# Encoder layer on one core: loads where the MLP begins, low parts of the activations, and the second product block by block

## The chip, the cores and the metric

The kernel runs on one core of one Trainium2 chip. The metric is the device time of one execution in microseconds (us). Before the change the median of three runs is 1813.73 us (1812.82 to 1814.87).

The engines are named as the profile names them: PE is TensorE's matmul stream, PEld its weight loads, DVE is VectorE, ACT is ScalarE, POOL is GpSimd and SP is SyncE, which issues all DMA transfers here.

## The reference, cut to what matters

One encoder layer is applied to two groups of tokens, 512 and 1024 of them, with shared weights, all in float32.

```python
def _layer(h, ...):
    a = _rmsnorm(h, norm_mix_g)
    z = a @ w_in                                  # queries, keys, values, pooling input
    ...
    h = h + jnp.concatenate([o_attn, o_pool], axis=-1) @ w_out
    m = _rmsnorm(h, norm_mlp_g)
    h = h + jnp.square(jax.nn.relu(m @ w_up)) @ w_down      # 1024 -> 4096 -> 1024
    gate = jax.nn.sigmoid(_rmsnorm(h, norm_ple_g) @ w_ple_gate)
    h = h + gate * (p_i @ w_ple_proj)
    return h
```

A final RMSNorm follows. The change touches the line of the MLP and what leads to it.

## The kernel before

**Tiles and stages.** The 1536 tokens are three chunks of 512 (c = 0, 1, 2). Activations stand transposed: 128 features on the partitions, tokens along the free dimension, so the residual `hT[c]` of a chunk is four tiles of [128, 2, 512]. Every float32 operand of a product is split into a high and a low part, and `three` gives the three matmuls high x high, high x low and low x high. The stages are: input projection (to about 196 us), attention and pooling with the output projection woven in (to 579 us), the MLP (to about 1620 us), the gate and the final norm.

**Buffers.** Nearly all tiles come from one pool of 49 buffers, `slot`. A tile takes a buffer that an earlier tile has left, and its first writer then waits for the last reader of that earlier tile. Where that reader was a DMA, the writer waits for the DMA's semaphore. PE, ACT, DVE and POOL run their instructions in the order in which the code is written. SP's queue is put in order when the program is built. Its transfers count on eight semaphores in turn, DMAHW0 to DMAHW7, and each transfer waits for the one eight places earlier.

**Ahead of the MLP.** `heads_out(p)` adds the output projection of a block of 256 tokens to `hT` (L755); p = 4 and 5 belong to chunk 2 and are the last of the stage. When a chunk is done, the chore `spill(c)` writes `hT[c]` to DRAM (`h_d`, L708), for chunk 2 after 16 empty steps. The chore `make_m(c)` (L595) reads it back, prepares the operand `mo` of the up product and the mean square of the rows plus epsilon, a [128, 512] tile that here is called the divisor `w`; L647 writes that to DRAM (`w_d`). Chores are generators: `step()` runs one of them by one step.

**The MLP.** A `Pair` (c, g) handles two of the 32 blocks of 128 hidden features for one chunk; 16 pairs for each chunk. Its up product uses seven products instead of eight (a Strassen form): `product(i)` for i = 1, 6, 2, 5, 7, 3, 4 with weight parts w1 to w7 and banks `px`, `py`, `pz`, `pq`. DVE reads the banks into u2 (L858), u4 (L866) and the activations c1, c2 (L870, L874, L880). Products 3 and 4 add onto `pz` and `pq` and thus wait for those reads. ACT takes relu and square and gives the high part of the activations r (L876, L882); DVE subtracts for the low part (L886). `down(a)` (L828) is the second product: two output blocks e = 0, 1 of a bank pair `pd`, each summed over the pair's two input blocks f = 0, 1, and then added to `hT` (L837). The `down` calls of a pair run between the up products of the next one (`between`).

After each product, `after(i)` (L1204) runs one step each of `feeding`, `splits`, `raising` and the chores. `feeding` (the generator `stream` over `Pair.feed`) prepares the weight parts of later pairs: ACT casts the high part (L786), POOL subtracts for the low part (L787), DVE makes the sums s1 to s4 (L793, L795, L801, L804). At i == 3 it issues the load of the next pair's up weights. `splits` does the same for the down weights (L816, L817: POOL for the first block, DVE for the second). `raising` (L658) multiplies `hT[c]` by `w`, in eight instructions, at the first pair of a chunk, since the MLP works on numbers without the norm's divisor. For it `load_ms(c)` reads `w_d` back. The chore `invert(c)` later takes the reciprocal and writes `w_d` again; the chore `finishing(c)` (L1131) multiplies by it, squares the result (L1142) for the next norm and scales it (L1126) for the gate.

The lines that set the place of the instructions around the change:

```python
            for e in range(2):                     # down, L830
                d = 2 * a + e
                for f in range(2):
...
            after(4)                               # run, L884
            for i, x in enumerate((c1, c2)):
                ve.tensor_tensor(self.r[i][:, 1], x, as32(self.r[i][:, 0]), op=ALU.subtract)
            between(3)
...
            if raising:                            # after, L1207
                next(raising, None)
```

## Time and profile before

| what | number |
|---|---|
| median of three runs | 1813.73 us |
| the profiled execution | 1813.31 us |
| its span | 1811.5 us |
| granted clock of TensorE, mean of the span | 0.995 |
| VectorE, ScalarE, GpSimd busy, share of the span | 70%, 52%, 58% |
| DMA, mean over the span | 142 GB/s |
| first matmul of the MLP | 579.01 us |

The page gives the busy time of each engine and, for groups of equal instructions, the idle time of the engine just ahead of them with what ended it. The list of waits sums such idle times by who waited for whom. The timeline shows the instructions of one engine in order of time: start, duration, line, operation, tiles, and in brackets the idle time ahead of it and its releaser. A table by stretches gives busy times, granted clock and DMA rate between two points of time. All times count from the start of the span.

### The profile page before, as it was taken

What the parts mean: (1) busy time and instruction counts of PE and PEld (TensorE: products, weight loads), DVE (VectorE), ACT (ScalarE), POOL (GpSimd) and SP (SyncE); (2) the same over time, 40 slices, a digit from 0 to 9 for tenths busy, and PEclk for the clock granted to TensorE, in tenths of its full rate; (3) what the DMA queues carried; (4) which work ended last, traced back from release to release, by engine and by line L of the source; (5) the groups of instructions that cost most, each with busy time, mean ns of one, the idle gap of its engine ahead of it and who ended that gap; (6) DMA issues with size and microseconds to landing.
All of it is one profiled execution on the core that took longest, in us unless ns stands there. A gap on an engine that the chain in (4) does not pass through costs nothing.

```text
span 1811.5 us, 28604 instructions
## 1 busy us (share of the span) xinstructions
PE 1759.7 (97%) x10540; PEld 1537.1 (85%) x10540; DVE 1260.0 (70%) x1843; ACT 939.7 (52%) x1854; POOL 1053.7 (58%) x923
## 2 busy tenths in 40 slices
PE   9999899999999799999999999999999999999997
PEld 7888777888868798988888889889898999888887
DVE  5677865888894677865568877876776556665655
ACT  6434455768794455655445545554455444443332
POOL 3474774535674567676656776785577666543121
PEclk9999999999999899999999999999999999999998
DMA  6333545120519335343364442556443323272102
GB/s 248 114 123 105 216 165 185 36 94 13 206 46 367 139 122 198 121 177 100 136 265 157 163 151 96 195 185 235 179 157 100 110 94 99 89 262 70 59 12 82
DMA packets 83883, 256.84 MB, mean 142 GB/s; under 512 B 9888, under 2 KB 16416, under 8 KB 83744
## 3 DMA queue, kind: packets, MB, share of 16 engines
q1 hardware_dynamic: 83744, 255.02, 39.7%
q8 instruction: 83, 1.36, 0.3%
q14 instruction: 56, 0.46, 0.1%
HBM read 195.74 MB, written 59.24 MB: 141 GB/s over the span
## 4 chain that ended last, share of the span: by engine, by line
PE 78%; DVE 7%; ACT 5%; DMA 3%; issue 3%; POOL 1%; POOLq 0%; DVEq 0%; ACTq 0%; SPq 0%
PE pd L49 25%; PE z L49 7%; PE px L49 6%; PE pz L49 6%; PE pq L49 6%; PE pg L49 6%; PE py L49 4%; PE pp L49 3%; PE o L49 3%; PE tp L53 3%; PE po L49 3%; PE S L49 3%; PE pj L49 1%; DMA wur<-in_w_up_dram 1%; DVE r L886 1%
## 5 line engine op out<-in xcount | busy, mean ns | idle before, releaser
L49 PE MATMUL pd<-r,wd 128*128 128x512 f32 x2304 | 568.5, 395 | 10.8 <-DVE r L886 10.6
L49 PEld LDWEIGHTS pd<-r,wd 128*128 128x128 f32 x2304 | 419.5, 188 | 100.3 <-DVE r L886 16.1
L787 POOL TENSOR_TENSOR w<-ws,w 128x512 fp32r<-128x512 f32 x192 | 272.5, 1423 | 217.9 <-ACT w L786 206.8
L787 POOL TENSOR_TENSOR w<-wur,w 128x512 fp32r<-128x512 f32 x144 | 212.8, 1489 | 135.4 <-ACT w L786 134.4
L837 DVE TENSOR_TENSOR h<-pd,h 128x1024 f32<-128x1024 f32 x192 | 233.5, 1216 | 76.6 <-PE pd L49 76.5
L786 ACT CAST w<-ws 128x512 fp32r<-128x512 f32 x192 | 118.5, 617 | 271.1 <-DVE ws L795 241.1
L461 POOL TENSOR_SCALAR pr<-pr,rr 128x512 f32<-128x512 f32 x160 | 111.2, 705 | 134.7 <-DVE rr L456 66.8
L49 PE MATMUL z<-w,x 128*128 128x512 f32 (+1 forms) x864 | 175.7, 359 | 0.9 <-DVE w L160 0.5
L49 PEld LDWEIGHTS pz<-mo,w 128*128 128x128 f32 x1152 | 150.7, 190 | 19.3 <-issue 11.2
L49 PEld LDWEIGHTS z<-w,x 128*128 128x128 f32 x864 | 142.9, 189 | 28.0 <-ACT w L159 2.1
L49 PE MATMUL pz<-mo,w 128*128 128x256 f32 x1152 | 153.6, 283 | 10.2 <-issue 10.2
L817 DVE TENSOR_TENSOR wd<-wdr,wd 128x512 fp32r<-128x512 f32 x96 | 102.8, 1071 | 83.1 <-ACT wd L816 76.6
L49 PE MATMUL pq<-mo,w 128*128 128x256 f32 x1152 | 153.7, 283 | 1.0 <-issue 1.0
L49 PE MATMUL px<-mo,w 128*128 128x256 f32 x1152 | 152.2, 281 | 0.0
L49 PEld LDWEIGHTS px<-mo,w 128*128 128x128 f32 x1152 | 146.5, 189 | 4.0
L49 PEld LDWEIGHTS pq<-mo,w 128*128 128x128 f32 x1152 | 144.7, 191 | 1.4 <-issue 1.3
L49 PE MATMUL pg<-hg,wg 128*128 128x512 f32 (+1 forms) x768 | 141.0, 338 | 0.2
L472 ACT CAST pt<-tp 128x512 fp32r<-128x512 f32 x160 | 88.0, 591 | 88.5 <-PE tp L53 86.8
L49 PEld LDWEIGHTS pg<-hg,wg 128*128 128x128 f32 x768 | 118.6, 188 | 17.8 <-DVE hg L1128 1.0
L817 POOL TENSOR_TENSOR wd<-wdr,wd 128x512 fp32r<-128x512 f32 x96 | 131.8, 1373 | 2.6 <-DMA w_d<-sqm 2.6
L886 DVE TENSOR_TENSOR r<-c,r 128x512 fp32r<-128x512 f32 x96 | 74.7, 783 | 74.1 <-ACT c L883 46.2
L473 DVE TENSOR_TENSOR pt<-tp,pt 128x512 fp32r<-128x512 f32 x160 | 104.0, 684 | 31.4 <-ACT pt L472 31.1
(195 smaller groups left out, 3036.2 us busy)
## 6 DMA issues: line engine op xcount, KB each, us to landing
wur<-in_w_up_dram SPq DMA_DIRECT2D x96, 512.0 KB, 4.2
wdr<-in_w_down_dram SPq DMA_DIRECT2D x96, 512.0 KB, 4.4
mo_d<-mm SPq DMA_DIRECT2D x84, 256.0 KB, 2.3
mo<-mo_d SPq DMA_DIRECT2D x42, 512.0 KB, 7.7
h_d<-h SPq DMA_DIRECT2D x16, 512.0 KB, 3.0
h<-h_d SPq DMA_DIRECT2D x16, 512.0 KB, 9.9
xn<-in_xn_dram SPq DMA_DIRECT2D x12, 512.0 KB, 6.4
qs_d<-qs SPq DMA_DIRECT2D x12, 512.0 KB, 3.0
```

The lines of the kernel that those rows point to most:

```text
L49: last_pe[0] = nc.tensor.matmul(*a, **k).ins
L53: last_pe[0] = nc.tensor.transpose(*a, **k).ins
L461: gp.tensor_scalar(p, p, rr, 1.0, op0=ALU.mult, op1=ALU.mult)
L472: sc.copy(self.pt[kt][:, 0], tp)
L473: ve.tensor_tensor(self.pt[kt][:, 1], tp, as32(self.pt[kt][:, 0]), op=ALU.subtract)
L786: sc.copy(t[:, 0], x)
L787: gp.tensor_tensor(t[:, 1], x, as32(t[:, 0]), op=ALU.subtract)
L817: (gp, ve)[i].tensor_tensor(lo, self.dr[i][:, h], as32(hi), op=ALU.subtract)
L837: ve.tensor_tensor(h, pd.rearrange("p (a b) -> p a b", a=2), h, op=ALU.add)
L886: ve.tensor_tensor(self.r[i][:, 1], x, as32(self.r[i][:, 0]), op=ALU.subtract)
```

## The change

It has four parts.

1. Where the MLP begins: the divisor of chunk 0 stays on the chip (`ws[0] = acc[:, 1]`) and is neither written to DRAM nor read back at that point; the up weights of the second pair are loaded ahead of chunk 0's `hT`, and no longer in `feeding`; chunk 2's `hT` is written to DRAM tile by tile as soon as its last sum is done, without the chore; and `raising` takes two steps after products 2, 5, 7, 3 and 4, and none after 1 and 6, in chunk 0.
2. In `run`, the two subtractions for the low parts of r stand ahead of `after(4)`.
3. In `down`, the loop over the input blocks f is the outer one.
4. In `finishing`, squaring and scaling go by halves, with a step after each.

```diff
--- before.py
+++ after.py
@@ -644,7 +644,10 @@
         for i in range(2):
             pe.matmul(bc, ones_sb, sh[:, i], start=i == 0, stop=i == 1)
         ve.tensor_scalar(acc[:, 1], bc, 1.0 / D, EPS, op0=ALU.mult, op1=ALU.add)
-        sy.dma_start(w_d[c], acc[:, 1])
+        if c:
+            sy.dma_start(w_d[c], acc[:, 1])
+        else:
+            ws[0] = acc[:, 1]
 
     def load_mo(c, i):
         MO[c, i] = [slot([P, 4, HF], F32R, f"mo{c}_{i}{j}") for j in range(2)]
@@ -703,7 +706,6 @@
     away = set()
 
     def spill(c):
-        yield from wait(16 if c == 2 else 0)
         for a in range(4):
             sy.dma_start(h_d[c][a], hT[c][a])
         away.add(c)
@@ -753,7 +755,10 @@
                     for i, (w_, x_) in enumerate(three(ws, [x[:, k, :] for x in cat[p]])):
                         pe.matmul(po, w_, x_, start=k == 0 and i == 0, stop=k == 3 and i == 2)
                 ve.tensor_tensor(h, po, h, op=ALU.add)
-                if d == KD - 1 and p % 2:
+                if p == 5:
+                    if d % 2:
+                        sy.dma_start(h_d[c][d // 2], hT[c][d // 2])
+                elif d == KD - 1 and p % 2:
                     chores.append(spill(c))
                     if c == 0:
                         chores.append(make_m(0, gp, gp))
@@ -827,9 +832,9 @@
 
         def down(self, a):
             pd = ps("d", f"pd{self.id}{a}")
-            for e in range(2):
-                d = 2 * a + e
-                for f in range(2):
+            for f in range(2):
+                for e in range(2):
+                    d = 2 * a + e
                     ws_ = [w[:, d * P:(d + 1) * P] for w in self.wd[f]]
                     for i, (w_, x_) in enumerate(three(ws_, [self.r[f][:, 0], self.r[f][:, 1]])):
                         pe.matmul(pd[:, e * CH:(e + 1) * CH], w_, x_, start=f == 0 and i == 0, stop=f == 1 and i == 2)
@@ -881,9 +886,9 @@
             sc.activation(c2, c2, AF.Relu)
             sc.activation(self.r[1][:, 0], c2, AF.Square)
             sc.activation(c2, c2, AF.Square)
-            after(4)
             for i, x in enumerate((c1, c2)):
                 ve.tensor_tensor(self.r[i][:, 1], x, as32(self.r[i][:, 0]), op=ALU.subtract)
+            after(4)
             between(3)
 
     NG = NF // 2
@@ -893,7 +898,7 @@
 
         for n, pr in enumerate(pairs):
             for i, _ in enumerate(pr.feed()):
-                if i == 3 and n + 1 < len(pairs):
+                if i == 3 and 0 < n < len(pairs) - 1:
                     pairs[n + 1].load_up()
                 yield
     feeding = stream()
@@ -1067,6 +1072,7 @@
 
     pairs[0].load_down()
     load_mo(0, ORDER[5]), load_mo(0, ORDER[6])
+    pairs[1].load_up()
     for a in range(4):
         load_h(0, a, h_d[0][a])
     while fill:
@@ -1139,10 +1145,11 @@
                 yield
             sy.dma_start(hl_d[c][a], h)
             sq = slot([P, 2, CH], F32, f"sqg{c}{a}") if a else acc
-            sc.activation(sq, h, AF.Square)
-            if c == 0:
-                gate_in(0, a, True)
-            yield
+            for e in range(2):
+                sc.activation(sq[:, e], h[:, e], AF.Square)
+                if c == 0:
+                    gate_in(0, a, True, (e,))
+                yield
             for e in range(2) if a else ():
                 gp.tensor_tensor(acc[:, e], acc[:, e], sq[:, e], op=ALU.add)
                 yield
@@ -1184,7 +1191,7 @@
             if c:
                 for a in range(4):
                     load_h(c, a, h_d[c][a])
-            load_ms(c)
+                load_ms(c)
             raising = raise_h(c)
         if g == 1:
             chores.append(invert(c))
@@ -1204,7 +1211,7 @@
         def after(i):
             next(feeding, None)
             next(splits, None)
-            if raising:
+            for _ in range(0 if not raising else 1 if c else 0 if i in (1, 6) else 2):
                 next(raising, None)
             if g == NG - 1 and c < 2:
                 load_mo(c + 1, i)
```

**The order at the start of the MLP, SyncE's queue.** Ahead of these rows stand the loads of `mo`, the up product's operand, for both programs alike. `h` from `h_d_0` to `h_d_3` in the 30x tiles is chunk 0 being read; `h_d` in the 31x tiles is chunk 2 being written; `wur` and `wdr` are raw up and down weights. Before:

```order
L56 DMA h_6357<-h_d_0_304 128x1024
L56 DMA h_6359<-h_d_1_305 128x1024
L56 DMA h_6361<-h_d_2_306 128x1024
L56 DMA h_6363<-h_d_3_307 128x1024
L647 DMA w_d_259<-sqm_4189 128x512
L708 DMA h_d_0_312<-h_5526 128x1024
L708 DMA h_d_1_313<-h_5528 128x1024
L708 DMA h_d_2_314<-h_5530 128x1024
L56 DMA wur_10_6531<-in_w_up_dram 128x1024
L56 DMA wur_11_6532<-in_w_up_dram 128x1024
L56 DMA w_6556<-w_d_259 128x512
L708 DMA h_d_3_315<-h_5532 128x1024
```

Now:

```order
L56 DMA wur_10_6357<-in_w_up_dram 128x1024
L56 DMA wur_11_6358<-in_w_up_dram 128x1024
L56 DMA h_6361<-h_d_0_304 128x1024
L56 DMA h_6363<-h_d_1_305 128x1024
L56 DMA h_6365<-h_d_2_306 128x1024
L56 DMA h_6367<-h_d_3_307 128x1024
L760 DMA h_d_0_312<-h_5526 128x1024
L760 DMA h_d_1_313<-h_5528 128x1024
L760 DMA h_d_2_314<-h_5530 128x1024
L760 DMA h_d_3_315<-h_5532 128x1024
L56 DMA wdr_10_6626<-in_w_down_dram 128x1024
L56 DMA wdr_11_6627<-in_w_down_dram 128x1024
```

The write and the read of `w_d` are gone from here, the second pair's up weights have moved ahead of the loads of `h`, and the four writes of chunk 2 stand together behind those.

**The same place, VectorE.** `ws` are the sums for the weight parts, `wd` the low part of the down weights; the raises are the instructions that multiply `h`. Before:

```order
L662 TENSOR_TENSOR h_6357<-h_6357,w_6556 128x512
L858 TENSOR_TENSOR u_0_6558<-py_0_6587,u_0_6558 128x256
L662 TENSOR_TENSOR h_6357<-h_6357,w_6556 128x512
L817 TENSOR_TENSOR wd_011_6583<-wdr_01_6346,wd_010_6582 128x512
L662 TENSOR_TENSOR h_6359<-h_6359,w_6556 128x512
L866 TENSOR_TENSOR u_0_6558<-pz_0_6630,u_0_6558 128x256
L793 TENSOR_TENSOR ws_10_6644<-wur_11_6532 128x512
L817 TENSOR_TENSOR wd_011_6583<-wdr_01_6346,wd_010_6582 128x512
```

Now:

```order
L863 TENSOR_TENSOR u_0_6559<-py_0_6587,u_0_6559 128x256
L822 TENSOR_TENSOR wd_011_6584<-wdr_01_6346,wd_010_6583 128x512
L665 TENSOR_TENSOR h_6361<-h_6361,sqm_4189 128x512 x2
L871 TENSOR_TENSOR u_0_6559<-pz_0_6630,u_0_6559 128x256
L798 TENSOR_TENSOR ws_10_6644<-wur_11_6358 128x512
L822 TENSOR_TENSOR wd_011_6584<-wdr_01_6346,wd_010_6583 128x512
L665 TENSOR_TENSOR h_6363<-h_6363,sqm_4189 128x512 x2
L875 TENSOR_TENSOR c_0_6560<-pq_0_6654,u_0_6559 128x256
```

u2 now stands ahead of all raises, the raises multiply by `sqm` itself, and the subtraction for `wd_011` and two raises stand ahead of u4 (the instruction that reads `pz`).

**The same place, ScalarE, with the semaphores waited for.** From the read of `px` (relu of the first pair) to the relu of c1. Before:

```order
L861 ACTIVATE c_0_6559<-px_0_6562 128x256 [waits PE_49]
L786 CAST w_0_4_6620<-wur_01_6098 128x512 [waits DMAHW1_49]
L816 CAST wd_010_6582<-wdr_01_6346 128x512 [waits DMAHW3_49]
L786 CAST w_1_1_6646<-wur_10_6531 128x512 [waits DMAHW0_49,Pool_49]
L816 CAST wd_010_6582<-wdr_01_6346 128x512
L786 CAST w_1_6_6668<-ws_10_6644 128x512 [waits DVE_49]
L875 ACTIVATE c_0_6559<-c_0_6559 128x256 [waits DVE_49]
```

Now:

```order
L866 ACTIVATE c_0_6560<-px_0_6563 128x256 [waits PE_49]
L791 CAST w_0_4_6619<-wur_01_6098 128x512 [waits DMAHW1_49]
L821 CAST wd_010_6583<-wdr_01_6346 128x512 [waits DMAHW6_49,DMAHW3_49]
L791 CAST w_1_1_6646<-wur_10_6357 128x512 [waits DMAHW0_49]
L821 CAST wd_010_6583<-wdr_01_6346 128x512
L791 CAST w_1_6_6669<-ws_10_6644 128x512 [waits DVE_49]
L880 ACTIVATE c_0_6560<-c_0_6560 128x256 [waits DVE_49]
```

The cast of `wd_010` now waits for DMAHW6 as well. In SyncE's queue above, the transfer that counts on that semaphore is the write of `h_d_0_312`, the first tile of chunk 2.

**The second product, TensorE.** From the end of the first product of the second pair to the end of the first `down`; r_00 and r_01 are the activations of the input blocks f = 0 and 1, with their high and low parts. Before:

```order
L49 MATMUL px_1_6724<-mo_10_6101,w_1_1_6646 128x256
L49 MATMUL pd_00_6748<-r_00_6560,wd_000_6580 128x512 x2
L49 MATMUL pd_00_6748<-r_00_6560,wd_001_6581 128x512
L49 MATMUL pd_00_6748<-r_01_6561,wd_010_6582 128x512 x2
L49 MATMUL pd_00_6748<-r_01_6561,wd_011_6583 128x512
L49 MATMUL pd_00_6748<-r_00_6560,wd_000_6580 128x512 x2
L49 MATMUL pd_00_6748<-r_00_6560,wd_001_6581 128x512
L49 MATMUL pd_00_6748<-r_01_6561,wd_010_6582 128x512 x2
L49 MATMUL pd_00_6748<-r_01_6561,wd_011_6583 128x512
L49 MATMUL py_1_6762<-mo_60_6190,w_1_6_6668 128x256
```

Now:

```order
L49 MATMUL px_1_6725<-mo_10_6101,w_1_1_6646 128x256
L49 MATMUL pd_00_6750<-r_00_6561,wd_000_6581 128x512 x2
L49 MATMUL pd_00_6750<-r_00_6561,wd_001_6582 128x512
L49 MATMUL pd_00_6750<-r_00_6561,wd_000_6581 128x512 x2
L49 MATMUL pd_00_6750<-r_00_6561,wd_001_6582 128x512
L49 MATMUL pd_00_6750<-r_01_6562,wd_010_6583 128x512 x2
L49 MATMUL pd_00_6750<-r_01_6562,wd_011_6584 128x512
L49 MATMUL pd_00_6750<-r_01_6562,wd_010_6583 128x512 x2
L49 MATMUL pd_00_6750<-r_01_6562,wd_011_6584 128x512
L49 MATMUL py_1_6764<-mo_60_6190,w_1_6_6669 128x256
```

Of each three, the second takes the low part of r. Before, the fourth to sixth matmul use block 1, with its low part at the fifth place; now block 1 comes from the seventh on, with its low part at the eighth.

## The prediction

> **What bounds the kernel now.** I read the page first, then the list of TensorE's waits, then the timelines of the engines around the longest of them. Of the page only the line of TensorE matters: it is busy for 97% of the span, so the change can only win what TensorE loses by waiting or by a lower clock. The list of waits (us in total, times, longest) names the two largest losses:
>
> ```profile
> PE 1759.7 (97%) x10540; PEld 1537.1 (85%) x10540; DVE 1260.0 (70%) x1843; ACT 939.7 (52%) x1854; POOL 1053.7 (58%) x923
> ...
> PE pd L49 <- DVE r L886: 10.6, 11, 1.8
> PE pz L49 <- issue: 10.2, 3, 9.2
> ```
>
> The second is nearly one wait, of 9.2 us. The timeline of TensorE (start, duration; in brackets the idle time before and its releaser) puts it where the MLP begins, with two waits of the first kind right behind it:
>
> ```profile
> 584.71 1.57 PE L49 MATMUL pq<-mo,w 128*128 128x256 f32 x12
> 595.48 2.90 PE L49 MATMUL pz<-mo,w 128*128 128x256 f32 x12 [9.20 <-issue]
> ...
> 604.34 0.96 PE L49 MATMUL pd<-r,wd 128*128 128x512 f32 x3 [1.77 <-DVE r L886]
> 606.04 2.12 PE L49 MATMUL pd<-r,wd 128*128 128x512 f32 x8 [0.74 <-DVE r L886]
> ```
>
> "issue" names no releaser, but the code does: product 3 adds onto the bank `pz`, which VectorE must first have read into u4 (L866). VectorE's timeline shows why that was late: its first raise of h stood 11.38 us for the divisor `w`, read back from memory, and u4 is queued behind three raises.
>
> ```profile
> 592.22 0.69 DVE L662 TENSOR_TENSOR h<-h,w 128x512 f32<-128x512 f32 x1 [11.38 <-DMA w<-w_d]
> ...
> 594.96 0.42 DVE L866 TENSOR_TENSOR u<-pz,u 128x256 f32<-128x256 f32 x1
> ...
> 598.97 1.70 DVE L662 TENSOR_TENSOR h<-h,w 128x512 f32<-128x512 f32 x1
> ...
> 603.61 2.38 DVE L886 TENSOR_TENSOR r<-c,r 128x512 fp32r<-128x512 f32 x2
> 598.84 1.28 POOL L787 TENSOR_TENSOR w<-ws,w 128x512 fp32r<-128x512 f32 x1 [6.54 <-ACT w L786]
> ```
>
> The table by stretches (busy us of PE, PEld, DVE, ACT, POOL, then granted clock, DMA share, GB/s) shows two more things of the same place: the DMA engines are full up to 595, and the clock is at half from about 590.6 (0.56 over five us) to 600.8 (0.92).
>
> ```profile
> 585.00:590.00 5.00, 1.28 (x11) 1.08 (x10) 0.00 (x0) 0.00 (x0) 4.55 (x4) 1.00 1.03 411
> 590.00:595.00 5.00, 0.00 (x0) 0.00 (x0) 2.78 (x6) 1.14 (x2) 1.64 (x2) 0.56 1.03 419
> 595.00:600.00 5.00, 4.52 (x21) 4.55 (x22) 5.00 (x10) 1.50 (x3) 1.16 (x1) 0.50 0.27 107
> 600.00:605.00 5.00, 3.23 (x21) 2.74 (x20) 4.70 (x6) 4.81 (x10) 2.87 (x3) 0.92 0.62 196
> ```
>
> **The change part by part. 1: the start of the MLP.** The divisor of chunk 0 is no longer written and read back, so the 11.38 us wait for `w` is gone. What is late next? The order of the queues answers. On ScalarE the first cast of the second half of the down weights (`wd_010`) now waits for a transfer on the semaphore DMAHW6: its buffer is the one that the first spilled tile of chunk 2 leaves. VectorE's next instruction waits for that cast, and behind it stand two raises and u4. So the first spill's landing takes the place of the divisor's. When does it land?
>
> ```profile
> 569.53 4.11 SPq L56 DMA_DIRECT2D h<-h_d  x4
> 575.93 0.32 SPq L647 DMA_DIRECT2D w_d<-sqm  x1
> ...
> w_d<-sqm SPq DMA_DIRECT2D x1, 256.0 KB, 9.4
> ```
>
> The write of `w_d` was issued at 575.93 and landed 9.4 later, at 585.3. It has 256 KB, 0.63 us at the 415 GB/s of the stretches; so the last load of h ahead of it landed at 584.7. In the new order two loads of up weights (512 KB, 1.27 us each) stand ahead of the four loads of h, and the first spill directly behind them: it lands at 584.7 + 3 x 1.27 = 588.5. From there: the cast, 0.62 as its kind takes on ScalarE, until 589.1; on VectorE the subtraction for `wd` and two raises at a pitch of 0.60 and u4 at 0.42, which is 2.2, until 591.4. But GpSimd starts its part of the next pair's first weight at 589.8, and the rows at 598.84 and 598.97 show what that costs: a raise that met a GpSimd instruction took 1.70 instead of 0.69, to just behind its end. One such meeting is a near tie here, so I take 592.0, between 591.4 and 592.4. TensorE then waits from 586.2 to 592.0 and gets 3.5 of the 9.2 back. The half clock remains: before it began 4.4 us after the last matmul and ended 5.3 us after the next one; a gap of 5.7 us still covers that, and a loss of 5.3 x 0.5 = 2.65 us stays in both.
>
> Behind it, 14 instructions of VectorE lead from u4 to the second r, before as after: before 5 raises and s3, now 6 raises (two in each of the calls after products 2, 5, 7 and 3) and no s3. So r comes as long after the start as before, 10.6 us, and only the new order of the second product helps there (part 2, 0.7). **Term: 3.5 + 0.7 = 4.2 us.** Bounds: 2.1 where a second raise meets GpSimd and the order gains nothing, and 6.6 where none meets it (4.1) and both waits of 1.77 and 0.74 go.
>
> Loading the next up weights ahead delays the loads of h by 2.5 us: the first then lands at about 583.4, ahead of 589.1, so it costs nothing as long as the spill is the later one; were it not, each us would cost one. The spills by themselves cost SyncE 0.32 us each, as before.
>
> **2: the second product block by block.** The twelve matmuls of `pd` need the low part of the second r first at the fifth place; now at the eighth. The rows of an undisturbed block give 2.78 us for twelve, so three are 0.70 us.
>
> ```profile
> 1018.20 2.94 PE L49 MATMUL pd<-r,wd 128*128 128x512 f32 x12
> 1020.98 1.58 PE L49 MATMUL pz<-mo,w 128*128 128x256 f32 x12
> ...
> 947.22 2.12 PE L49 MATMUL pd<-r,wd 128*128 128x512 f32 x8 [0.72 <-DVE r L886]
> 990.34 2.14 PE L49 MATMUL pd<-r,wd 128*128 128x512 f32 x8 [0.75 <-DVE r L886]
> 1013.37 2.13 PE L49 MATMUL pd<-r,wd 128*128 128x512 f32 x8 [1.46 <-DVE r L886]
> 1036.50 2.15 PE L49 MATMUL pd<-r,wd 128*128 128x512 f32 x8 [1.52 <-DVE r L886]
> 1145.08 2.12 PE L49 MATMUL pd<-r,wd 128*128 128x512 f32 x8 [1.54 <-DVE r L886]
> 1296.00 2.13 PE L49 MATMUL pd<-r,wd 128*128 128x512 f32 x8 [0.76 <-DVE r L886]
> 1360.31 2.13 PE L49 MATMUL pd<-r,wd 128*128 128x512 f32 x8 [0.88 <-DVE r L886]
> ```
>
> These seven waits are 7.63 us; with the two at the start, 2.51, the eleven of the list's 10.6 leave about 0.5 for the two smallest. Each wait gets up to 0.70 shorter: 7 x 0.70 + 0.5 = 5.4 us. Matmuls are neither added nor taken away, and VectorE reads the pair of banks after all twelve in both orders, so the order costs nothing.
>
> **3: squares by halves.** What is left of the waits at 1013 and 1036 (0.76 and 0.82) came from ScalarE. Its chain to r stood behind one square of 1.05 and two scaled copies of 1.32:
>
> ```profile
> 1005.73 1.05 ACT L1142 ACTIVATE sqg<-h 128x1024 f32<-128x1024 f32 x1
> 1006.69 1.32 ACT L1126 ACTIVATE hg<-h,gple_sb 128x512 fp32r<-128x512 f32 x2
> 1007.92 0.40 ACT L875 ACTIVATE c<-c 128x256 f32<-128x256 f32 x1
> ...
> 1012.05 1.26 DVE L886 TENSOR_TENSOR r<-c,r 128x512 fp32r<-128x512 f32 x1 [1.68 <-ACT c L883]
> ```
>
> They now come in two steps of about 1.2, and in the new order of ScalarE no pair of chunk 1 has more than one of them inside that chain. A wait of 1.5 less 0.7 less 1.2 is none. That gives 0.76 + 0.82 + 0.05 + 0.02 + 0.06 + 0.18 = 1.9; the 0.84 left at 1145 belongs to another chore (casts of the next chunk's operand), which now comes four steps later and may or may not meet the chain again; I leave it in. A square in two halves costs ScalarE little (an engine busy 52% of the span). **Term of parts 2 and 3: 5.4 + 1.9 = 7.3, I take 7.2;** bounds 5.4 (the halves gain nothing) and 8.1 (all nine waits go).
>
> **4: the low parts ahead of the last weight part.** On VectorE both subtractions for r now stand ahead of s3, which had filled the idle time before them:
>
> ```profile
> 1006.96 0.80 DVE L801 TENSOR_TENSOR ws<-wur,wur 128x512 f32<-128x512 f32 x1
> ...
> 1012.69 0.62 ACT L786 CAST w<-ws 128x512 fp32r<-128x512 f32 x1
> 1016.16 1.74 POOL L787 TENSOR_TENSOR w<-ws,w 128x512 fp32r<-128x512 f32 x1
> 1022.40 1.60 PE L49 MATMUL pq<-mo,w 128*128 128x256 f32 x12
> ```
>
> The wait at 1012.05 was for ScalarE, so r gains nothing from it: 0. Its price falls on weight 7: cast at 1012.69, subtracted until 1017.9, used at 1022.4, a slack of 4.5 us. s3 would now end some 0.8 to 1.2 after the second r, at about 1014, and hold that cast by about 1.3 us; the slack covers it. Without that cover it would be paid in some 46 pairs. The spill's chore of 16 empty steps is gone and the halves add four, so the chores of chunk 0 run earlier and the last of chunk 1 some 13 us later (4 of 7 steps in a pair of 23 us); nothing waits on them at present, 0.
>
> **Sum.** 4.2 + 7.2 = 11.4 us. The profiled execution took 1813.31 (a span of 1811.5 and 1.8 around it): 1801.9. The median of the runs lies 0.4 above it, so 1802.3, rounded to **1802**.
>
> **The rivals.** *The clock does not drop* (for it: the gap shrinks from 9.2 to 5.7; against it: the drop came 4.4 us after the last matmul). Without the half clock 2.65 more are won: 1799. The Trainium skill (TensorE: Matmul & The Clock Gate, Part 1: The HAM clock gate) says that the gate looks at windows of about 3.4 us that run freely, and halves the clock after one that is idle. By that rule the drop can come anywhere from 3.4 to 6.8 us after the last matmul, and a gap of 5.7 misses it about one time in three; the one drop seen here agrees, but cannot show the spread.
>
> *Another wait takes all of the start* (the spill lands late, or the raises that are now in pairs meet GpSimd each time at 1.0 more): the 4.2 are gone, 1806. For it: DMA is full there and VectorE's queue is just as long. Against it: the divisor had two transfers in a row to wait for, the spill one.
>
> *The chores land badly:* moved by some steps, they meet ScalarE's chain in other pairs, and of 7.2 only 3 remain, 1806 to 1810. For it: the wait at 1145 has such a cause.
>
> *The change does not do what it says:* the order of `pd` is plain in TensorE's queue, so only the 5.4 of it could fail, if r came later by what the order gains: 1813.
>
> *Slower:* s3 behind r delays weight 7 by more than the 4.5 us of slack. From there each us costs 46 us, so 0.25 us beyond it would eat the gain, and 0.35 make it 1818. Against it: the estimate of 1.3.
>
> **How the numbers follow.** The forecast has 0.53, the undropped clock 0.13, the start taken by another wait 0.15, the chores 0.10, no effect 0.05, slower 0.04. The range of 1797.5 to 1807 takes in the first three, 0.81, and the bounds: 2.1 + 5.4 gives 1806.2, and 6.6 + 8.1 gives 1799.0, with some room for the clock. A measurement here can tell about 0.2%, 3.6 us, from no change: faster is below 1810.1. Faster 0.89, same 0.07, slower 0.04.
>
> **What would show it.** In the profile after: the gap of `pz` at the start near 5.7 us with the wait of the first `wd` cast for a DMA of `h_d`; VectorE with no wait for `w<-w_d` at 592; the sum of `pd` waits for r near 1.5 instead of 10.6; no activation of 128x1024 among the squares of the finishing chore. Wrong it would be if the gap stays near 9, if `pd` still waits over 5 us in total, or if `pq` begins to wait for GpSimd in every pair.

## The result and the profile after

The changed kernel takes 1831.78 us (median of four runs, 1831.58 to 1831.99), the kernel before, run beside it, 1813.68 (1812.82 to 1814.87). The ratio is 1.0096, with an interval of 1.0084 to 1.0109: 18 us slower, where 11.4 us faster was forecast. The span of the profiled execution grew from 1811.5 to 1830.1.

The page's line of busy times and the list of TensorE's waits (us in total, times, longest), after:

```profile
PE 1769.6 (97%) x10540; PEld 1539.6 (84%) x10540; DVE 1329.4 (73%) x1843; ACT 944.1 (52%) x1862; POOL 1052.0 (57%) x923
...
PE pq L49 <- DVE c L875: 11.2, 9, 2.4
PE pd L49 <- DVE r L890: 7.8, 10, 1.3
PE pz L49 <- issue: 6.6, 3, 6.2
...
PE pz L49 <- DVE u L871: 2.3, 2, 1.2
```

The waits of `pz` without a releaser, nearly all at the start of the MLP, shrank (10.2 to 6.6), the waits of `pd` for r only from 10.6 to 7.8, and two waits are new: product 4 (`pq`) and product 3 (`pz`) wait for VectorE's reads of their banks. VectorE is busy 69 us longer with the same 1843 instructions. Which of them grew? The groups of equal instructions (busy us, mean ns; then the idle time ahead of them and its releasers), before and after:

```profile
L793 DVE TENSOR_TENSOR ws<-wur 128x512 f32<-128x512 f32 x48 | 44.4, 926 | 0.4 <-POOL w L787 0.4
L804 DVE TENSOR_TENSOR ws<-wur,ws 128x512 f32<-128x512 f32 x48 | 35.9, 748 | 0.0
L801 DVE TENSOR_TENSOR ws<-wur,wur 128x512 f32<-128x512 f32 x48 | 35.5, 739 | 0.0
```

```profile
L806 DVE TENSOR_TENSOR ws<-wur,wur 128x512 f32<-128x512 f32 x48 | 84.4, 1759 | 0.0
...
L809 DVE TENSOR_TENSOR ws<-wur,ws 128x512 f32<-128x512 f32 x48 | 63.1, 1314 | 0.0
L798 DVE TENSOR_TENSOR ws<-wur 128x512 f32<-128x512 f32 x48 | 54.3, 1131 | 6.7 <-POOL w L792 6.7
```

These are s1 (L793, now L798), s4 (L804, L809) and s3 (L801, L806). s3 went from 739 to 1759 ns on average over the 48 pairs. A pair without chores shows how, and what follows. (Pairs are counted from 1 within each chunk, and a pair here runs from the start of its product `py` to the next pair's.) This is pair 14 of chunk 0. GpSimd, before (`py` began at 862.36):

```profile
866.39 3.02 POOL L787 TENSOR_TENSOR w<-wur,w 128x512 fp32r<-128x512 f32 x2
...
880.55 3.07 POOL L787 TENSOR_TENSOR w<-ws,w 128x512 fp32r<-128x512 f32 x2 [1.07 <-ACT w L786]
```

The same after (`py` at 863.04), with VectorE's s3 and ScalarE's cast for weight 7:

```profile
868.16 3.00 POOL L792 TENSOR_TENSOR w<-wur,w 128x512 fp32r<-128x512 f32 x2
...
881.33 1.78 DVE L806 TENSOR_TENSOR ws<-wur,wur 128x512 f32<-128x512 f32 x1
...
883.14 0.62 ACT L791 CAST w<-ws 128x512 fp32r<-128x512 f32 x1 [1.18 <-DVE ws L806]
...
881.21 1.35 POOL L792 TENSOR_TENSOR w<-ws,w 128x512 fp32r<-128x512 f32 x1 [1.07 <-ACT w L791]
883.84 1.29 POOL L792 TENSOR_TENSOR w<-ws,w 128x512 fp32r<-128x512 f32 x1 [1.28 <-ACT w L791]
```

Behind both r, s3 starts just after GpSimd's subtraction for weight 5 (881.21 to 882.56) and ends 0.55 us behind that. Before, GpSimd does weights 5 and 7 without a gap; after, it stands 1.28 us between them, because s3 holds the cast. That repeats in every pair, so all that stands behind weight 7 comes later: GpSimd's row of weight parts ends 866.39 + 3.02 - 862.36 = 7.05 us behind `py` before, 868.16 + 3.00 - 863.04 = 8.12 after. This pair pays nothing for that (its period stays at 21.1 us). A pair with chores does. TensorE, VectorE and GpSimd in pair 4 of chunk 1, after (`py` at 994.15):

```profile
1005.47 1.57 PE L49 MATMUL pz<-mo,w 128*128 128x256 f32 x12
1008.82 2.54 PE L49 MATMUL pq<-mo,w 128*128 128x256 f32 x12 [1.79 <-DVE c L875]
...
1004.42 1.57 DVE L798 TENSOR_TENSOR ws<-wur 128x512 f32<-128x512 f32 x1
1005.91 1.77 DVE L822 TENSOR_TENSOR wd<-wdr,wd 128x512 fp32r<-128x512 f32 x1
1007.60 0.74 DVE L1134 SCALAR_TENSOR_TENSOR hg<-h,gple_sb,hg 128x512 fp32r<-128x512 f32 x1
1008.26 0.41 DVE L875 TENSOR_TENSOR c<-pq,u 128x256 f32<-128x256 f32 x1
...
1002.44 1.74 POOL L1154 TENSOR_TENSOR sqg<-sqg,sqg 128x512 f32<-128x512 f32 x1
1004.14 2.98 POOL L792 TENSOR_TENSOR w<-wur,w 128x512 fp32r<-128x512 f32 x2
```

And before, in the same pair (`py` at 992.32):

```profile
1001.47 1.57 DVE L793 TENSOR_TENSOR ws<-wur 128x512 f32<-128x512 f32 x1
1002.96 0.68 DVE L817 TENSOR_TENSOR wd<-wdr,wd 128x512 fp32r<-128x512 f32 x1
1003.56 0.68 DVE L1138 TENSOR_TENSOR h<-h,w 128x512 f32<-128x512 f32 x1
1004.16 0.41 DVE L870 TENSOR_TENSOR c<-pq,u 128x256 f32<-128x256 f32 x1
...
999.49 3.00 POOL L787 TENSOR_TENSOR w<-wur,w 128x512 fp32r<-128x512 f32 x2
```

Here the chores have filled both engines. Before, GpSimd's row ended at 1002.49, 10.17 us behind `py` and just ahead of `wd`, which took 0.68. After, it runs to 1007.12, 12.97 behind `py`; s1 meets it as before (1.57), `wd` now too (1.77), the read of `pq` into c2 is late, and product 4 waits 1.79 us for it. Not all of this lateness comes from the low parts: the sum `sqg` is a chore's, and two such sums stand ahead of the row's end in this pair where the kernel before has them elsewhere. The experiments tell the two apart. The granted clock then falls as well:

```profile
1005.00:1010.00 5.00, 3.21 (x22) 2.94 (x21) 5.00 (x7) 0.62 (x1) 2.13 (x2) 0.92 0.34 136
1010.00:1015.00 5.00, 5.00 (x23) 4.31 (x23) 2.97 (x5) 3.50 (x7) 2.58 (x2) 0.73 0.55 183
```

The start of the MLP went nearly as forecast: `pz` waits 6.18 us in place of 9.20, forecast 5.7. ScalarE and TensorE, after:

```profile
589.04 0.62 ACT L821 CAST wd<-wdr 128x512 fp32r<-128x512 f32 x1 [4.04 <-DMA h_d<-h]
...
593.11 2.90 PE L49 MATMUL pz<-mo,w 128*128 128x256 f32 x12 [6.18 <-issue]
...
600.84 1.68 PE L49 MATMUL pd<-r,wd 128*128 128x512 f32 x6 [1.28 <-DVE r L890]
603.08 1.43 PE L49 MATMUL pd<-r,wd 128*128 128x512 f32 x5 [0.56 <-DVE r L890]
```

So where did the time go? From the timeline of TensorE I took the start of `py` in each pair, counted from that of the first pair, and subtracted the same of the kernel before. This table holds it for fifteen kernels (us; negative is ahead of the kernel before), and in the last column where GpSimd's row ends behind `py` in the pairs 12 to 15 of chunk 0, which have no chores. The run first_pair below has no line, since its profiled execution was a slow one of 4446.68 us, as single ones of undo_low and of the kernel before were; ratios leave these out.

| kernel | pair 2 of chunk 0 | start of chunk 1 | start of chunk 2 | last pair | GpSimd's row |
|---|---|---|---|---|---|
| before | 0 | 0 | 0 | 0 | 7.0 to 7.2 |
| after | -4.3 | 0.2 | 15.7 | 17.6 | 8.1 to 8.2 |
| undo_low | -2.4 | -2.4 | 2.8 | 1.7 | 7.0 |
| only_low | -2.4 | -0.3 | 10.1 | 13.1 | 8.1 to 8.2 |
| only_start | -1.6 | -0.5 | -0.5 | 0.3 | |
| only_blocks | -0.6 | -0.8 | -2.4 | -3.6 | |
| start_blocks | -3.3 | -3.3 | -6.6 | -7.7 | 7.0 |
| only_halves | 1.3 | 1.7 | 10.6 | 10.8 | |
| phase_kept | -3.4 | -3.6 | -9.0 | -7.2 | |
| low_s3_early | -2.5 | -0.3 | 2.7 | 3.9 | 7.0 to 7.1 |
| lows_apart | -4.1 | -4.6 | -6.0 | -5.2 | 7.0 to 7.1 |
| first_halves | -4.3 | -4.8 | -6.5 | -7.5 | |
| w7_twice | -0.1 | 2.2 | 11.4 | 13.5 | 8.2 to 8.5 |
| late_w7 | -0.4 | 0.0 | 1.2 | 1.5 | 7.0 to 7.1 |
| halves_in_place | -4.7 | -5.1 | -10.8 | -11.9 | 7.0 to 7.1 |

The row "after" reads: 4.3 us won at the start, 4.5 lost in chunk 0, 15.5 in chunk 1, 1.9 in chunk 2. Chunk 1 has most of the chores.

### The profile page after: what moved, and what is told of

It is laid out like the page before. It is cut to its first block, busy times and chain, and to the rows that moved or that the text cites. A ratio compares the mean times of both kernels' runs of the same rounds, so it can differ in the third digit from the quotient of the medians.

```text
span 1830.1 us, 28602 instructions
## 1 busy us (share of the span) xinstructions
PE 1769.6 (97%) x10540; PEld 1539.6 (84%) x10540; DVE 1329.4 (73%) x1843; ACT 944.1 (52%) x1862; POOL 1052.0 (57%) x923
## 5 line engine op out<-in xcount | busy, mean ns | idle before, releaser
L792 POOL TENSOR_TENSOR w<-ws,w 128x512 fp32r<-128x512 f32 x192 | 256.9, 1338 | 258.5 <-ACT w L791 245.6
L49 PEld LDWEIGHTS pz<-mo,w 128*128 128x128 f32 x1152 | 151.0, 190 | 18.7 <-issue 10.8
L890 DVE TENSOR_TENSOR r<-c,r 128x512 fp32r<-128x512 f32 x96 | 70.5, 735 | 126.7 <-ACT c L888 83.9
L822 DVE TENSOR_TENSOR wd<-wdr,wd 128x512 fp32r<-128x512 f32 x96 | 109.2, 1138 | 59.6 <-ACT wd L821 43.0
L822 POOL TENSOR_TENSOR wd<-wdr,wd 128x512 fp32r<-128x512 f32 x96 | 147.9, 1541 | 0.0
```

Source lines behind the costliest of these rows:

```text
L49: last_pe[0] = nc.tensor.matmul(*a, **k).ins
L792: gp.tensor_tensor(t[:, 1], x, as32(t[:, 0]), op=ALU.subtract)
L822: (gp, ve)[i].tensor_tensor(lo, self.dr[i][:, h], as32(hi), op=ALU.subtract)
```

## The experiments

### One part taken out, one part alone

undo_low puts `after(4)` back ahead of r; only_low is the kernel before with r ahead of `after(4)`, and nothing else:

```diff
-            after(4)
             for i, x in enumerate((c1, c2)):
                 ve.tensor_tensor(self.r[i][:, 1], x, as32(self.r[i][:, 0]), op=ALU.subtract)
+            after(4)
             between(3)
```

> The changed kernel with one part undone: after(4) stands ahead of the two subtractions for r again. Theory Q (the order on VectorE: s3 behind r leaves VectorE idle and then meets GpSimd's subtraction in every pair, GpSimd gets its input late and has no time left in the pairs with chores): this takes back nearly all of what was lost, about 1802 us (1799 to 1806), with s3 near 740 ns on average instead of 1759 and no wait of pq for c. Theory C (the chores of the finishing and of make_m come some steps earlier or later and that is what costs): stays near 1831 (1826 to 1834). Theory B (the second product with f outside holds its banks or needs its weights at a bad time): stays near 1831 too.

> The kernel before with only the two subtractions for r put ahead of after(4). Theory Q: s3 goes from 739 to about 1750 ns, and the time rises by about as much as undo_low falls, 25 to 30 us: 1836 to 1844 us, for the chores of this kernel stand in about the same pairs. Theories C and B: no effect, 1812 to 1815.

undo_low: 1815.04 us, ratio to the kernel before 1.000 (0.999 to 1.0009). only_low: 1828.29, ratio 1.0075 (1.0062 to 1.0089), 13.6 us, half of the 25 to 30 that theory Q expected. So the low parts are the larger cost, but not all of it: undo_low stays 13 us above 1802, which no theory had. In its pairs 7, 10 and 14 of chunk 1 (24.2, 25.0 and 25.8 us long) instructions of the chores hold up what TensorE waits for. VectorE in pair 7:

```profile
1072.43 1.48 DVE L552 TENSOR_TENSOR dgg<-id_sb,rhg 128x512 fp32r<-128x512 f32 x2 [4.45 <-POOL rhg L548]
1073.83 0.42 DVE L885 TENSOR_TENSOR c<-pq,u 128x256 f32<-128x256 f32 x1
```

`dgg` stands near the end of the chore finishing. The read of `pq` stands right behind its wait of 4.45 us for GpSimd.

only_start has part 1 alone, only_blocks part 3 alone:

> The kernel before with only part 1 (the divisor on the chip, the up weights of the second pair ahead, chunk 2 written tile by tile, two raises per step). Theory Q: the start wins about 3.5 to 4.2 us and the rest stays, 1809 to 1811 us. Theory C: the 16 empty steps that are gone move the chores of chunk 0 and cost there what the traces show between pairs 4 and 5, about 4 us: 1812 to 1815.

> The kernel before with only the loop over f outside in down. Theory Q, and the prediction's second term: each of nine or ten waits of pd for r gets up to 0.70 us shorter, 1807.5 to 1809.5 us. Theory B: slower than 1816 us, with new waits of pd or of the instruction that adds pd to h.

only_start: 1814.13 us, ratio 0.9996 (0.9987 to 1.0005). only_blocks: 1809.71, ratio 0.997 (0.996 to 0.9981), 5.4 us, just the second term. Part 1 wins 1.6 us at the start and loses 1.1 of it in chunk 0; the time lies in the range of theory C, but of the 4 us that it puts between pairs 4 and 5 only some 1.3 are there. The waits of `pd` for r are 5.4 us in only_blocks, where they were 10.6.

### Do the parts add up?

start_blocks has parts 1 and 3; only_halves has part 4 alone.

> Parts 1 and 3 together (the start of the MLP and the loop over f outside in down); the low parts and the halves stay as before. Theory C2 (the two prices of the change are the low parts ahead of s3, and the four steps of the halves that put make_m of chunk 2 into other places of its pairs): the two parts add up, 0.7 and 5.4 us, so about 6 us below the kernel before of the same call, ratio 0.9967 (0.996 to 0.998). Theory I (the gain of the blocks is lost as soon as part 1 is there): no different from the kernel before, ratio 0.9995 to 1.001.

> The kernel before with only part 4, squares and scaled copies by halves. Theory C2: the waits of pd for r in chunk 1 shrink by about 2 us, but make_m of chunk 2 comes four steps later and costs about 8 us in the pairs 7, 10 and 14 of chunk 1 (undo_low lost 3.0, 3.9 and 4.8 there against its neighbours): 4 to 7 us above the kernel before, ratio 1.002 to 1.004. The prediction's third term: 1.9 us below, ratio 0.999.

start_blocks: 1807.39 us, ratio 0.9956 (0.9941 to 0.9971), some 2 us better than the sum expected. only_halves: 1823.45, ratio 1.0044 (1.0029 to 1.0059), 8 us slower, more than expected. In the last of its dear pairs GpSimd works without a gap, now with subtractions of make_m (L634) between those of the weights, and VectorE and TensorE wait. (In the first row, `wd` waits for a write of `mo_d`, a transfer of make_m too.)

```profile
1224.03 1.11 DVE L817 TENSOR_TENSOR wd<-wdr,wd 128x512 fp32r<-128x512 f32 x1 [4.46 <-DMA mo_d<-mm]
...
1235.20 1.77 DVE L801 TENSOR_TENSOR ws<-wur,wur 128x512 f32<-128x512 f32 x1 [1.91 <-POOL mm L634]
...
1238.70 0.96 PE L49 MATMUL pd<-r,wd 128*128 128x512 f32 x3 [2.33 <-DVE r L886]
```

By the four single runs the parts add up: 13.6 + 8.0 - 5.4 - 0.7 = 15.5 us, beside the 17.4 (0.0096 of 1813.7) of the whole.

### The place of the chores

phase_kept is undo_low with empty steps, so that each chore stands at the same place of a pair as before:

```diff
     def invert(c):
+        yield from wait(1 if c == 0 else 0)
...
-        yield from wait(6)
+        yield from wait(9)
         yield from spread_g(c, acc)
```

> As undo_low (parts 1, 3 and 4), with one empty step ahead of invert(0) and three more in finishing, so that every later chore stands in the same place of a pair as in the kernel before, one whole pair of seven steps earlier or later. The work is that of undo_low. Theory C2: the losses in pairs 7, 10 and 14 of chunk 1 are gone, and the parts add up to 1.6 to 2.4 us from the start and 7.2 from blocks and halves: 8.8 to 9.6 us below the kernel before, ratio 0.995. If the halves themselves cost, or the chores' place does not matter: like undo_low, ratio 1.000.

1807.49 us, ratio 0.9958 (0.9943 to 0.9972): four empty steps win 7.6 us over undo_low, some 1 to 2 less than expected. The dear pairs of chunk 1 are gone: 24.2, 25.0 and 25.8 us became 21.1 each, and one pair later, where these chores now stand, 22.5, 21.8 and 21.6. The table has it 9.0 ahead at the start of chunk 2. There it loses 3.3 in one pair, for make_m ends a whole pair later and the divisor of chunk 2 with it. VectorE and TensorE:

```profile
1275.65 0.69 DVE L665 TENSOR_TENSOR h<-h,w 128x512 f32<-128x512 f32 x1 [11.07 <-DMA w<-w_d]
...
1277.53 3.06 PE L49 MATMUL pd<-r,wd 128*128 128x512 f32 x12 [3.10 <-DVE h L843]
```

### What in the low parts costs

low_s3_early has the low parts first, but s3 one step earlier; lows_apart (with parts 1 and 3 and the empty step ahead of `invert(0)`) has s3 between the two (`low` is the subtraction for r):

```diff
             split(2, a12)
+            ve.tensor_tensor(s3, a11, a21, op=ALU.subtract)
             yield
             split(5, s1)
-            ve.tensor_tensor(s3, a11, a21, op=ALU.subtract)
             yield
```

```diff
+            low(0, c1)
             after(4)
-            for i, x in enumerate((c1, c2)):
-                ve.tensor_tensor(self.r[i][:, 1], x, as32(self.r[i][:, 0]), op=ALU.subtract)
+            low(1, c2)
```

> The kernel before with the two subtractions for r ahead of after(4), as in only_low, and with s3 written one step earlier (in after(3), ahead of the read of pq), where VectorE waits for product 4 anyway. Theory Q: it is s3 behind r that costs; here it is not behind r, so the 13 us of only_low go and some 2.4 us at the start of the MLP remain as a gain: ratio 0.998 to 1.000. If it is r itself, ahead of the rest, that costs: like only_low, ratio 1.0075.

> Parts 1 and 3 and the empty step, with the first low part ahead of after(4) and the second behind it, in all pairs: s3 stands again where VectorE waits for ScalarE. Theory Q: no price; s3 near 740 ns, w7 as early as before, ratio 0.994 to 0.997. If the low part of c1 ahead of s3 is itself what costs: about 13 us more than start_blocks, ratio 1.002 to 1.004.

low_s3_early: 1818.22 us, ratio 1.0014 (1.0005 to 1.0024); 11 of 13.6 us are gone, not all. lows_apart: 1809.09, ratio 0.997 (0.9959 to 0.9982), some 2.5 above start_blocks in place of 13. But I expected s3 near 740 ns there, and it is as slow as after:

```profile
L807 DVE TENSOR_TENSOR ws<-wur,wur 128x512 f32<-128x512 f32 x48 | 84.7, 1765 | 0.0
```

So the slow s3 is not itself the price. What sets lows_apart apart from the changed kernel is the last column of the table: there GpSimd's row ends at 7.0. Two more runs on the kernel before part the two things that are late behind s3. w7_twice makes GpSimd do its subtraction for weight 7 twice; late_w7 does weight 7 one step later, with other work in its place:

```diff
-                gp.tensor_tensor(t[:, 1], x, as32(t[:, 0]), op=ALU.subtract)
+                for _ in range(2 if i == 7 else 1):
+                    gp.tensor_tensor(t[:, 1], x, as32(t[:, 0]), op=ALU.subtract)
```

```diff
-            split(7, s3)
             ve.tensor_tensor(s4, a12, s2, op=ALU.subtract)
             yield
+            split(7, s3)
             split(3, s4)
```

> The kernel before, with GpSimd's subtraction for weight 7 done twice (the second time with the same result). VectorE's order is untouched; GpSimd's row of weight parts in each pair ends some 1.3 us later, about as late as with the low parts ahead of s3 (1.1 to 1.2 in a pair without chores). Theory G (the price of the low parts is that GpSimd's row of each pair ends later and then meets VectorE's s1, wd and the read of pq behind them): no cost in pairs without chores, and 8 to 15 us in the pairs with chores, mostly of chunk 1; ratio 1.004 to 1.008. Theory V (the price comes from VectorE's own order): at most 1 us, ratio 0.9995 to 1.0007.

> The kernel before, with cast and subtraction of weight 7 one step later (together with those of weight 3). GpSimd does the first low part of the down weights in the meantime, so its row ends about as early as before, but weight 7 itself comes some 2 us later. Theory G: no cost, ratio 0.9995 to 1.001. If weight 7 is the part that comes too late for its own product (the prediction's rival, 0.35 us beyond a slack in 46 pairs): 10 us or more, ratio above 1.005, with waits of pq for w.

w7_twice: 1830.27 us, ratio 1.0086 (1.0073 to 1.01). 15.6 us slower, with VectorE's order untouched, s3 at 765 ns, and mostly in the same pairs: 9.2 us of it in chunk 1, none in pairs without chores. It comes to the late row by added work, which only_low does without. late_w7: 1815.54, ratio 1.0004 (0.9995 to 1.0013). Its trace has two waits of product 7 for weight 7, 0.74 and 0.84 us, both in the first pair ahead of the long wait of `pz`, and none behind it. So weight 7 may be late; GpSimd's row may not.

The 16 pairs of chunk 1, where the chores are, bear this out. On average GpSimd's row ends there 9.0 us behind `py` in the kernel before and 10.3 in only_low, 10.8 in w7_twice, 9.3 in low_s3_early, 8.9 in late_w7; the chunk takes 10.4, 9.2, 3.0 and 1.2 us longer than before. (In all but w7_twice a stretch of half clock, 3.41 us long, is in that, which can cost 1.7; in late_w7 it comes behind a wait of 1.52 us that the kernel before has too.) lows_apart and start_blocks both have 9.5 and lie 1.9 us apart.

How the late row turns into time differs from pair to pair. In pair 4 of chunk 1 undo_low, which has the chores' two sums as the changed kernel does, ends the row 11.50 us behind `py`. So of the 2.80 us between 10.17 and 12.97 some 1.3 come with the chores' place and 1.5 with the low parts. In only_low, with the chores where they were, the row of that pair ends only 0.5 us later than before (`py` at 994.84), and s1 and `wd` behind u4 do not meet it:

```profile
1005.40 0.41 DVE L866 TENSOR_TENSOR u<-pz,u 128x256 f32<-128x256 f32 x1
1005.74 0.68 DVE L793 TENSOR_TENSOR ws<-wur 128x512 f32<-128x512 f32 x1
1006.33 0.68 DVE L817 TENSOR_TENSOR wd<-wdr,wd 128x512 fp32r<-128x512 f32 x1
...
1002.06 3.44 POOL L787 TENSOR_TENSOR w<-wur,w 128x512 fp32r<-128x512 f32 x2
```

There u4 itself is late, 10.56 us behind `py` where it was 8.82: VectorE's instructions ahead of it took longer.

### Versions without the two costs

first_pair has parts 1 and 3, the empty step ahead of `invert(0)`, and the low parts first only where `c == g == 0`. first_halves adds the halves, and takes as many steps out of finishing (GpSimd's two sums in one step, `wait(5)`). halves_in_place is phase_kept with the low parts first in the first pair alone, and with `wait(3 if c == 2 else 7)` ahead of the product that makes the divisor.

> Parts 1 and 3, with one empty step ahead of invert(0), and with the low parts ahead of after(4) in the first pair alone, where the raises and the low part of the down weights leave VectorE no idle time. Theory C2 and Q: the 7.7 us of start_blocks, 1.0 more at the start (4.29 in the changed kernel against 3.30 there) and 0.6 in pair 5 of chunk 0, together 9.3 us below the kernel before, ratio 0.9949. If the price of the low parts is paid in each pair from its first on and not by meetings with GpSimd, one pair of 48 costs 0.3 and the gain at the start stays: much the same; so this run is for the sum of the parts, not for the cause.

> As first_pair, with squares and scaled copies by halves and as many steps taken out of finishing (GpSimd's two sums in one step, five empty steps instead of six), so that make_m of chunk 2 stands where it stood before. Theory C2: the halves then gain the 1.9 us of the prediction over first_pair, 1.3 to 2.2, and chunk 2 does not lose the 3 us that it lost in phase_kept: ratio 0.9938. If the halves gain nothing, or GpSimd's two sums in a row cost as much: as first_pair, ratio 0.995.

> As phase_kept, with the low parts ahead of after(4) in the first pair alone, and with three empty steps in place of seven ahead of the product that makes the divisor of chunk 2, which came 3.3 us too late for chunk 2 in phase_kept. If the halves' gain in pairs 3 to 5 of chunk 1 (3.3 us over start_blocks) is theirs: 7.7 of phase_kept, 0.9 at the start and 3 in chunk 2, 11.6 us below the kernel before, ratio 0.9936 (0.993 to 0.9945). If it is given back in other pairs wherever the chores stand: as first_pair, 0.995.

first_pair: 1805.52 us, ratio 0.9951 (0.9938 to 0.9965), as expected. first_halves: 1807.16, ratio 0.9962 (0.9949 to 0.9974): in that form the halves gain nothing. halves_in_place: 1802.07, ratio 0.993 (0.9916 to 0.9943), 12.7 us faster than before and the fastest measured. Its longest waits in the MLP:

```profile
PE pz L49 <- issue: 6.9, 3, 5.8
PE pd L49 <- DVE r L892: 2.0, 3, 1.1
```

It holds all four edits, the low parts first in one pair of 48, and the chores where they were. That is the time which was forecast for the change as it stands, but of another program and from other terms, so the match is partly luck.

## Why the prediction was wrong, point by point

The prediction numbers the parts in its own way: its 2 is the second product (part 3 of the change), its 3 the halves (part 4) and its 4 the low parts (part 2). Its numbers stand here.

**The step that failed: 4, the low parts.** "s3 would now end some 0.8 to 1.2 after the second r, at about 1014, and hold that cast by about 1.3 us; the slack covers it." The hold was right: 1.28 us of idle time on GpSimd, though s3 ended 1.7 behind the second r, since it met GpSimd and took 1.78 instead of the 0.80 of before. So was the slack of weight 7: late_w7 makes it late and costs next to nothing. What failed is that I followed the late instruction only to its own user. Behind weight 7 in GpSimd's queue stand the parts of weights 3 and 4, of the next pair's weight 1, and of the down weights. They all moved by 1.1 us in a quiet pair. In pairs with chores there was no room for that: VectorE's instructions ahead of its reads of the banks met GpSimd and the reads came late. The prediction had put this at nothing. only_low prices the step at 13.6 us, and that is after the 2.4 that the low parts win at the start. low_s3_early, with the row nearly on time, gets back 11 of these 13.6, and w7_twice shows that a late row is enough for such a price. The slack had been read in one pair, from one instruction.

**A second step failed in the same paragraph:** the four steps of the halves, "nothing waits on them at present, 0". Nothing waits for the chores, but their instructions stand in the queues of VectorE and GpSimd ahead of others that are waited for. Alone that is 8.0 us (only_halves), and the four empty steps of phase_kept took 7.6 off undo_low.

**1, the start.** 4.2 forecast, 4.29 in the trace, and the landing of the first spill ended the wait, as the order of the queues said. But the shares were wrong, and the match is partly luck. The wait for `pz` shrank by 9.20 - 6.18 = 3.0, not 3.5. The two waits of `pd` for r went from 1.77 and 0.74 to 1.28 and 0.56, 0.7 less. The half clock, which was to cost 2.65 in both, got cheaper: 5.3 us of it lay behind the wait before, and 3.1 after (it ends at 596.23), which by half is an estimate of 1.1 us won. And the start isn't the same each time: the kernel before and only_halves do the same there and take 27.6 and 28.9 us from the first `py` to the second. start_blocks and undo_low, with the same edits there too, win 3.3 and 2.4. In undo_low and in only_start, which wins 1.6, a second stretch of half clock, 3.41 us long, follows the wait of `pd`; start_blocks has none. So what each edit won of the 4.29 is known to about 1 us only.

Alone, part 1 gave 1.1 back in chunk 0. Without the 16 empty steps the chores stand eight steps earlier there, one more than a whole pair of seven. With that one step put back, pair 5 of chunk 0 takes 21.1 us in phase_kept and lows_apart, where it took 21.7 in start_blocks and 22.4 in only_start. The clock did fall at the start, so the rival without a half clock did not come true.

**2, the second product.** 5.4 forecast, 5.4 by the times of only_blocks (0.997, with an interval of 3.4 to 7.3 us). The mechanism is in the list of waits: those of `pd` for r fell from 10.6 to 5.4. The one trace of only_blocks, its slowest execution, shows 3.6 between the first and the last pair, so the agreement to 0.1 us is luck.

**3, the halves.** 1.9 forecast. In pairs 3 to 5 of chunk 1 phase_kept is 3.3 us faster than start_blocks, more than forecast; in all, halves_in_place stands some 3.8 us below first_pair (0.993 beside 0.9951, each with about 0.0014 either way). Both also move steps of the chores, and first_halves, which moves them otherwise, gains nothing. So the gain is that of the halves together with their steps' place; the halves' own wasn't measured.

**The rivals.** "Slower" named the right instruction, s3 behind r, but weighed it by the slack of weight 7. "The chores land badly" named the second cause, and let it take some 4 of the 7.2 us won; alone the halves took 8.0. Both had their place in the text; neither was followed down the queue of the engine that has it.

**Left open.** Why lows_apart stays 2.5 us above start_blocks and low_s3_early 2.5 above the kernel before (5 with what it wins at the start): in both GpSimd's row is on time in the pairs without chores. For lows_apart 1.7 of it stands in the first pair of chunk 2, where `pd` waits 1.75 us for r; why r is late there wasn't followed. Which of VectorE's instructions carry the price in each dear pair wasn't tried apart either. In chunk 1 of only_low s1 takes no longer in all than before (17.5 us for 16), `wd` 38.2 in place of 35.5 and s4 17.8 in place of 11.9.

## What to carry to other kernels

When an instruction moves later, follow every instruction behind it on each engine that it feeds, not only its own user, and read their room in the fullest pair, not in a quiet one. Work that "nothing waits for" still takes its place in queues that others wait in: if an edit adds steps to it, keep the phase (here a whole pair of seven steps) or count it as moved everywhere. And where a saving has no wait to take away, as the low parts had almost only in the first pair, make it only where the wait is.

## What the runs showed of the hardware

An instruction of VectorE on two 128x512 operands that met GpSimd's row took 1.77 in place of 0.68 us, to 0.55 us behind GpSimd's end. GpSimd's sum that began while VectorE was busy took 1.74 (at 1002.44), where its instructions of that size take 1.29 (at 883.84); the one that began ahead of s3 took 1.35 (at 881.21). So an engine that comes late into another's busy time can stretch its own work and the other's.

The half clock does not need an idle TensorE for the whole of a window. In the records of the granted clock its stretches, but for the one that the end of the span cuts off, are 3.41 us or two or three times that. After the wait of 1.79 us above there is one of 3.41 us; another after a wait of 2.31. I cut the span of the fifteen kernels into windows of 3.41 us from such edges. Every window with 1.9 us or more without a matmul was followed by half clock, and none with less than 1.4; between them both occur. So the longest wait after the change behind the start of the MLP, 2.39 us and split by an edge, cost no clock, and one of 1.79 cost some 1.7 us more (half of 3.41). The Trainium skill (TensorE: Matmul & The Clock Gate, Part 1: The HAM clock gate) tells of windows of that length and of one idle window; the length agrees, but here about half a window was enough.
